# A decoder layer's kernel: the third group's sum of squares made earlier, the first two groups' norms and the third's operands in smaller steps of a held order

## The chip, the core and the metric

The kernel runs on one core of a Trainium2 chip. The metric is the time of one execution on the device in microseconds (us). The core has a matrix engine (TensorE, here PE, with PEld for the loading of its weights), a vector engine (VectorE, DVE), a scalar engine (ScalarE, ACT), a general engine (GpSimd, POOL), and a queue (SyncE, SP) that here issues nearly all transfers (DMA) between device memory and the core's memory.

## What is computed

One layer of a decoder over 2048 tokens of width 1024. A projection feeds a gated linear recurrence (HGRN2, 4 heads of 128) and a stick-breaking attention (8 heads of 64); each half's output is normalised, and both go through one output projection. A feed-forward network (FFN) and a gated embedding follow.

```python
def reference(x, p, attn_pre_norm, w_in, ...):
    h = x
    ...
        u = rmsnorm(h, attn_pre_norm[i])
        proj = u @ w_in[i]
        ...
        o_hg = hgrn2_mix(hq, hf, hi, lb_all[i])
        o_hg = rmsnorm(o_hg.astype(x.dtype), hg_out_norm[i]) * jax.nn.silu(hg)
        o_sb = stick_breaking_mix(...).reshape(B, T, SB_WIDTH)
        o_sb = rmsnorm(o_sb, sb_out_norm[i])
        mix = jnp.concatenate([o_hg, o_sb], axis=-1) @ w_out[i]
        h = h + rmsnorm(mix, attn_post_norm[i])
        u = rmsnorm(h, ffn_pre_norm[i])
        gate, up = jnp.split(u @ w_gate_up[i], [D_FF], axis=-1)
        y = (jax.nn.silu(gate) * up) @ w_down[i]
        h = h + rmsnorm(y, ffn_post_norm[i])
        h = h + (p[i] @ ple_proj[i]) * jax.nn.sigmoid(h @ ple_gate[i])
    return h
```

The change touches what lies around `mix` and the two lines after it: the sum of squares of `o_sb`, the operands of the output projection, and the norm behind it.

## The kernel before

The tokens are worked in four groups of 512 (`NG`), each as four tiles of 128 (`TT`). A product in 32-bit floats is made of three passes of PE (`mm3`, L221 to L223): the high part of one operand with the high part of the other, and the two mixed ones. `split` (L207, L208) makes the two parts: a cast on ACT gives the high part (`uh`, `wh`), and a subtraction on DVE or POOL (`V`, `G`) the low one (`ul`, `wl`).

The order of PE is that of the code; the stages are generators (`Stream`) that are woven into each other, a step at a time, by `weave` and `Rate`: of `(rows, 3, 1)` three steps are taken over the slots of that call. The instructions of the other engines and of SP are ordered by a scheduler, which works from the code's order and its own estimates. A call in `pin(...)` holds its instruction behind the one that was written before it for the same engine.

The stages that matter here, in order of time, with the places of the profiled execution:

- The last recurrence projection (to 1157 us): the input projection of group 3, with attention and the recurrence of group 2 (`hgrn(2)`) woven in, and the stream `loads[0]`, which fetches group 0's output (`out_load`).
- The output projections of groups 0 (1157 to 1252) and 1 (1252 to 1344), `out_proj`. Into them are woven the last attention, the recurrence of group 3 (`hgrn(3)`), in the second one also `post_mix(0)` (norm and residual of group 0) and `first_rows(2)`, which makes the first operands for group 2.
- The pair (1344 to 1437), `out_pair(2)`: the output projections of groups 2 and 3 in one, by seven products instead of eight; the products come in the order 1, 2, 6, 3, 7, 5, 4. `post_mix(1)` is woven in, and `first_operands`, which prepares the FFN.

The recurrence works by levels: chunks of 64 rows are halved again and again, and at each level POOL (`qp`) and DVE (`ks`) update two factors (L579, L581), and PE multiplies them (L542, L553); ACT copies the results (`score`, L566, L573). L448 and L452 are steps of the attention on DVE and POOL.

`square_sums` (L763 to L769) loads a tile of the attention's output (`o_s`), squares it on ACT (L766 the first into the sum `oss`, L768 the others) and adds it on POOL (L769). `tile_sums` (L774, L776) brings the sums of 512 tokens over rows into 4 columns, and `ratio` (L782 to L786) makes of them and of the recurrence's sums (`hgss`) the scale of one half against the other, in six small operations on POOL. `over_rows` (L792, L794) spreads the ratio over the partitions, and `scaled` (L798) multiplies an operand with it. In `first_rows`, `raw` is loaded (L808 the recurrence's half) and split. In `post_mix`, each tile has a norm in DVE (L938, two halves, after POOL's L273 and L276 for the root) and an addition (L939, DVE for the first half, POOL for the second) to the residual `h`; a second norm (ACT's L943) gives the FFN's input, which PE transposes (L949), ACT evicts (L953, four pieces each) and SP stores (L955). In the pair, `w_prep` (L837 to L846) brings weights and `a_prep` the operands; their combinations are made by L1086 and L1089, loads come by L1058, and other splits are L1073 and L1074.

Two pools bound what can be under way: `xt` has 8 buffers of 128x512, `ev` 12.

Of the kernel before, what the change touches and what calls it, by code (L numbers as in the profile page):

```python
# [13 lines left out]
ALU = mybir.AluOpType  # L14
# [76 lines left out]
def hybrid_block(  # L91
# [91 lines left out]
    def ev(dt=F32, name="ev", shape=(P, GT)):  # L183
        return fb.tile(list(shape), dt, tag="ev", name=name, bufs=12)
# [576 lines left out]
    def square_sums(acc, first, g, ks, new):  # L761
        for k in ks:
            raw = new()  # L763
            nc.sync.dma_start(raw, o_s[g][HH + k])
            if k == first:
                nc.scalar.activation(acc, raw, AF.Square)  # L766
            else:
                nc.scalar.activation(raw, raw, AF.Square)  # L768
                nc.gpsimd.tensor_tensor(acc, acc, raw, op=ALU.add)  # L769
# [27 lines left out]
    def scaled(k, raw, r):  # L797
        nc.vector.scalar_tensor_tensor(raw, raw, g_sb[:, k:k + 1], r, op0=ALU.mult, op1=ALU.mult)  # L798

    def first_rows(g, tt):  # L800
        acc = ev(name="oss")
        square_sums(acc, 0, g, range(HH), xt)
        yield
        r = ratio(g, tile_sums(acc))
        yield
        for k in range(HH):
            raw = xt("raw")
            nc.sync.dma_start(raw, o_s[g][k])  # L808
            tt[1, k] = split(wpool, "u", UB, raw, V if k % 2 else G)
            if k % 2:  # L810
                yield
        r = over_rows(r, "tr", xt)
        yield
        for k in range(HH):
            raw = xt("raw")
            nc.sync.dma_start(raw, o_s[g][HH + k])
            scaled(k, raw, r)
            nc.sync.dma_start(on_s[k], raw)
            tt[2, k] = split(wpool, "u", UB, raw, V if k % 2 else G)
            if k % 2:  # L820
                yield
# [105 lines left out]
    def post_mix(g, mix, tags, new):  # L927
# [3 lines left out]
        for t in range(TT):  # L931
            hs = [xt("h"), xt("h")]
            for j in range(2):
                nc.sync.dma_start(hs[j], x[g * GT + t * P:g * GT + (t + 1) * P, j * GT:(j + 1) * GT])
            r = row_rstd(mix[t])
            for j in range(2):
                d = mix[t][j]
                nc.vector.scalar_tensor_tensor(d, d, r, gb[j], op0=ALU.mult, op1=ALU.mult)  # L938
                (nc.gpsimd if j else nc.vector).tensor_tensor(hs[j], hs[j], d, op=ALU.add)  # L939
                nc.sync.dma_start(h_s[g][t * P:(t + 1) * P, j * GT:(j + 1) * GT], hs[j])  # L940
            r = row_rstd(hs)
            for j in range(2):
                nc.scalar.activation(mix[t][j], hs[j], AF.Copy, scale=r)  # L943
            yield
# [552 lines left out]
    loads = [Stream(out_load(g, res[g])) for g in range(2)]  # L1497
    spent = 11
    for n, (kind, g, att_n, hg_n) in enumerate(plan):
# [12 lines left out]
            0: (kept_out, 14), 2: (kept_out, 14), 4: (kept_ffn, 16), 5: (kept_ffn, 16), 6: (loads[0], ND)}.get(n, (idle, 0))  # L1512
# [28 lines left out]
    for g in range(2):  # L1541
# [6 lines left out]
        else:  # L1548
            rows = Stream(first_rows(2, tto))
            weave(op, 4, rates.part(4), r3.part(4), (pm, TT, 0), (rows, 3, 1))  # L1550
            weave(op, 2, rates.part(2), r3.part(2))
            acc3 = ev(name="oss")
            square_sums(acc3, 0, 3, range(HH - 1), xt)
            weave(op, 2, rates.part(2), r3.part(2), (pm, TT // 2, 0))
            att_stream.drain()
            square_sums(acc3, 0, 3, (HH - 1,), xt)
            weave(op, 3, r3.part(3), (pm, TT, 0), (rows, 1, 1))
            ss3 = tile_sums(acc3)
            weave(op, 2, r3.part(2), (pm, TT // 2, 0), (rows, 1, 1))
            hgs[3].drain()  # L1560
            rr3 = ratio(3, ss3)
            weave(op, 3, (rows, 2, 1))
# [19 lines left out]
    weave(op, 4, (pm, TT, 0))  # L1582
# [76 lines left out]
```

## Time and profile before

| what | value |
| --- | --- |
| median of 3 runs | 2965.28 us (2963.56 to 2966.44) |
| the profiled execution | 2966.78 us |
| its span, from first to last instruction | 2965.0 us |
| mean granted clock of PE | 0.992 |
| PE busy | 2862.4 us, 97% |
| DVE, ACT, POOL busy | 71%, 53%, 47% |
| output projection of group 1 (1252 to 1344): PE busy | 75.40 of 92 us |

A group's line in the profile has the line of the kernel, the engine, the operation, its output and inputs, the shapes and the count; behind the bar stand the busy time, the mean of one in ns, and the idle time before it with what ended it. A row in order of time begins with its start and its duration in us; in brackets stands how long the engine was idle before it and which engine, name and line ended that. "Waits" list how long an engine waited for what: in total, how often, and the longest.

### The profile page before, as it was taken

What the parts mean: (1) busy time and instruction counts of PE and PEld (TensorE: products, weight loads), DVE (VectorE), ACT (ScalarE), POOL (GpSimd) and SP (SyncE); (2) the same over time, 40 slices, a digit from 0 to 9 for tenths busy, and PEclk for the clock granted to TensorE, in tenths of its full rate; (3) what the DMA queues carried; (4) which work ended last, traced back from release to release, by engine and by line L of the source; (5) the groups of instructions that cost most, each with busy time, mean ns of one, the idle gap of its engine ahead of it and who ended that gap; (6) DMA issues with size and microseconds to landing.
All of it is one profiled execution on the core that took longest, in us unless ns stands there. A gap on an engine that the chain in (4) does not pass through costs nothing. (4 is left out here: it accounts for less than half of the span.)

```text
span 2965.0 us, 51986 instructions
## 1 busy us (share of the span) xinstructions
PE 2862.4 (97%) x17796; PEld 2397.8 (81%) x17796; DVE 2114.2 (71%) x3051; ACT 1581.2 (53%) x3220; POOL 1387.7 (47%) x1384
## 2 busy tenths in 40 slices
PE   9999999999999999988999999999999999999999
PEld 7878888877888788877788778788888888888777
DVE  4776777777788777756977777756877765666685
ACT  5667657666667666765623333455433233545542
POOL 3345456545665666764433211355722121456653
PEclk9999999999999999999999999999999999999999
DMA  7785576456556454448986787867965555677975
GB/s 230 234 257 169 173 222 207 143 168 211 182 184 183 147 155 131 142 146 310 331 283 211 253 275 265 269 204 226 325 217 174 177 172 174 214 221 236 329 253 168
DMA packets 487561, 635.27 MB, mean 214 GB/s; under 512 B 45184, under 2 KB 275584, under 8 KB 487296
## 3 DMA queue, kind: packets, MB, share of 16 engines
q1 hardware_dynamic: 487296, 631.95, 67.5%
q8 instruction: 141, 2.31, 0.3%
q14 instruction: 124, 1.02, 0.1%
HBM read 459.29 MB, written 172.49 MB: 213 GB/s over the span
## 5 line engine op out<-in xcount | busy, mean ns | idle before, releaser
L1073 ACT CAST wh<-wr 128x512 fp32r<-128x512 f32 x592 | 347.1, 618 | 501.0 <-PE mm L222 110.5
L1074 POOL TENSOR_TENSOR wl<-wr,wh 128x512 fp32r<-128x512 f32 x256 | 370.2, 1454 | 439.8 <-ACT wh L1073 390.6
L452 POOL TENSOR_TENSOR a<-be,ring 128x512 f32<-128x512 f32 (+2 forms) x320 | 325.5, 1018 | 410.0 <-DVE ring L448 382.9
L1074 DVE TENSOR_TENSOR wl<-wr,wh 128x512 fp32r<-128x512 f32 x336 | 303.4, 911 | 159.4 <-ACT wh L1073 136.4
L221 PE MATMUL mm<-uh,wh 128*128 128x512 f32 x968 | 401.4, 415 | 7.9 <-DVE vv L365 4.4
L223 PE MATMUL mm<-uh,wl 128*128 128x512 f32 x968 | 380.5, 393 | 0.0
L222 PE MATMUL mm<-ul,wh 128*128 128x512 f32 x968 | 380.2, 393 | 0.0
L448 DVE TENSOR_TENSOR_SCAN ring<-z,ring,be 128x512 f32<-128x512 f32 x192 | 245.6, 1279 | 88.2 <-ACT z L434 83.5
L221 PE MATMUL mm<-wh,uh 128*128 128x256 f32 (+1 forms) x840 | 262.4, 312 | 2.9 <-DVE eb L351 2.2
L222 PE MATMUL mm<-wl,uh 128*128 128x256 f32 (+1 forms) x840 | 249.4, 297 | 4.1 <-POOL wl L208 2.6
L223 PE MATMUL mm<-wh,ul 128*128 128x256 f32 (+1 forms) x840 | 248.7, 296 | 0.0
L433 ACT ACTIVATE be<-z 128x512 f32<-128x512 f32 (+2 forms) x320 | 171.1, 535 | 100.6 <-DVE z L431 60.9
L465 DVE TENSOR_TENSOR al<-tr,ah 128x512 fp32r<-128x512 f32 (+1 forms) x320 | 191.6, 599 | 43.7 <-ACT ah L463 42.1
L221 PEld LDWEIGHTS mm<-uh,wh 128*128 128x128 f32 x968 | 183.5, 190 | 43.4 <-issue 3.8
L223 PEld LDWEIGHTS mm<-uh,wl 128*128 128x128 f32 x968 | 182.5, 189 | 41.2
L207 ACT CAST wh<-wr 128x512 fp32r<-128x512 f32 x256 | 158.6, 619 | 102.4 <-PE mm L222 51.1
L463 ACT CAST ah<-tr 128x512 fp32r<-128x512 f32 (+1 forms) x320 | 167.8, 524 | 84.6 <-PE tr L460 83.0
L208 POOL TENSOR_TENSOR wl<-wr,wh 128x512 fp32r<-128x512 f32 x128 | 171.5, 1340 | 78.8 <-ACT wh L207 58.7
L222 PEld LDWEIGHTS mm<-ul,wh 128*128 128x128 f32 x968 | 183.4, 190 | 30.4
L460 PE MATMUL tr<-ident,a 128*128 128x128 f32 x1088 | 178.4, 276 | 19.5 <-POOL a L452 19.5
L427 PE MATMUL z<-kt,q 128*128 128x512 f32 (+3 forms) x640 | 189.4, 377 | 0.0
L1074 POOL TENSOR_TENSOR wl<-s,wh 128x512 fp32r<-128x512 f32 x40 | 62.2, 1557 | 269.8 <-ACT wh L1073 224.9
(387 smaller groups left out, 7598.3 us busy)
## 6 DMA issues: line engine op xcount, KB each, us to landing
wr<-in_w_gate_up_dram SPq DMA_DIRECT2D x292, 256.0 KB, 4.3
wr<-in_w_in_dram SPq DMA_DIRECT2D x224, 256.0 KB, 3.3
wr<-hid_s SPq DMA_DIRECT2D x154, 256.0 KB, 3.1
wr<-in_w_down_dram SPq DMA_DIRECT2D x110, 256.0 KB, 3.6
wr<-h_s SPq DMA_DIRECT2D x96, 256.0 KB, 4.5
wr<-wd_s SPq DMA_DIRECT2D x88, 256.0 KB, 3.1
kt<-k_s SPq DMA_DIRECT2D x80, 256.0 KB, 3.2
vt<-v_s SPq DMA_DIRECT2D x80, 256.0 KB, 3.3
```

The lines of the kernel that those rows point to most:

```text
L208: (lo_engine or nc.gpsimd).tensor_tensor(lo, src, hi.bitcast(F32), op=ALU.subtract)
L221: nc.tensor.matmul(o, l[0], r[0], start=start, stop=False)
L222: nc.tensor.matmul(o, l[0], r[1], start=False, stop=False)
L223: nc.tensor.matmul(o, l[1], r[0], start=False, stop=stop)
L427: nc.tensor.matmul(z[:, :n], st["q"][i][:, tb * P:(tb + 1) * P], ch["k"][:, :n], start=i == 0, stop=i == 1)
L433: nc.scalar.activation(be[:, :n], z[:, :n], AF.Sigmoid, scale=0.125)
L448: nc.vector.tensor_tensor_scan(r[:, o:o + n][:, ::-1], z[:, :n][:, ::-1], be[:, :n][:, ::-1], init, op0=ALU.mult, op1=ALU.bypass)
L452: nc.gpsimd.tensor_tensor(a[:, :n], be[:, :n], r[:, o + 1:o + n + 1], op=ALU.mult)
L460: nc.tensor.transpose(tr[:, tb * P:(tb + 1) * P], ch["a"][tb][:, sb * P:(sb + 1) * P], ident)
L465: nc.vector.tensor_tensor(lo[:, lo_c:], tr[:, lo_c:], hi[:, lo_c:].bitcast(F32), op=ALU.subtract)
L1073: nc.scalar.copy(hi, src)
L1074: lo_engine.tensor_tensor(lo, src, hi.bitcast(F32), op=ALU.subtract)
```

## The change

- A new generator `row_sums` makes the sum of squares of a group's attention output in four steps of one tile each and a fifth for the sums over rows. That of group 2 runs in the stream of the last recurrence projection, behind `out_load(0)`; the stream there takes 13 steps instead of 8. That of group 3 stays in the output projection of group 1, and its sum lies in a buffer of `xt` instead of `ev`.
- `first_rows` begins with the ratio, and makes its four operands and its four scaled operands in single steps, not in pairs.
- The squares (L766, L768), the high part of the recurrence's operands, the scalings (L798) and the norm (L938) are pinned.
- `post_mix` has three steps for each tile's norm instead of one, within the same slots; its transposes begin two slots earlier.

No instruction is added or removed on any engine.

```diff
@@ square_sums
-                nc.scalar.activation(acc, raw, AF.Square)
+                pin(nc.scalar.activation(acc, raw, AF.Square))
             else:
-                nc.scalar.activation(raw, raw, AF.Square)
+                pin(nc.scalar.activation(raw, raw, AF.Square))
                 nc.gpsimd.tensor_tensor(acc, acc, raw, op=ALU.add)
...
     def scaled(k, raw, r):
-        nc.vector.scalar_tensor_tensor(raw, raw, g_sb[:, k:k + 1], r, op0=ALU.mult, op1=ALU.mult)
+        return nc.vector.scalar_tensor_tensor(raw, raw, g_sb[:, k:k + 1], r, op0=ALU.mult, op1=ALU.mult)
+
+    sums = {}
+
+    def row_sums(g, new):
+        acc = new("oss")
+        for k in range(HH):
+            square_sums(acc, 0, g, (k,), xt)
+            if k < HH - 1:
+                yield
+        yield
+        sums[g] = tile_sums(acc)
 
     def first_rows(g, tt):
-        acc = ev(name="oss")
-        square_sums(acc, 0, g, range(HH), xt)
-        yield
-        r = ratio(g, tile_sums(acc))
+        r = ratio(g, sums[g])
         yield
         for k in range(HH):
             raw = xt("raw")
             nc.sync.dma_start(raw, o_s[g][k])
-            tt[1, k] = split(wpool, "u", UB, raw, V if k % 2 else G)
-            if k % 2:
-                yield
+            tt[1, k] = split(wpool, "u", UB, raw, V if k % 2 else G, placed=pin)
+            yield
         r = over_rows(r, "tr", xt)
         yield
         for k in range(HH):
             raw = xt("raw")
             nc.sync.dma_start(raw, o_s[g][HH + k])
-            scaled(k, raw, r)
+            pin(scaled(k, raw, r))
             nc.sync.dma_start(on_s[k], raw)
             tt[2, k] = split(wpool, "u", UB, raw, V if k % 2 else G)
-            if k % 2:
-                yield
+            yield
...
@@ post_mix, first loop over the tiles
             r = row_rstd(mix[t])
+            yield
             for j in range(2):
                 d = mix[t][j]
-                nc.vector.scalar_tensor_tensor(d, d, r, gb[j], op0=ALU.mult, op1=ALU.mult)
+                pin(nc.vector.scalar_tensor_tensor(d, d, r, gb[j], op0=ALU.mult, op1=ALU.mult))
                 (nc.gpsimd if j else nc.vector).tensor_tensor(hs[j], hs[j], d, op=ALU.add)
                 nc.sync.dma_start(h_s[g][t * P:(t + 1) * P, j * GT:(j + 1) * GT], hs[j])
+                if j == 0:
+                    yield
...
-    loads = [Stream(out_load(g, res[g])) for g in range(2)]
+    def last_loads():
+        yield from out_load(0, res[0])
+        yield from row_sums(2, lambda name: ev(name=name))
+
+    loads = [Stream(last_loads()), Stream(out_load(1, res[1]))]
...
-            0: (kept_out, 14), 2: (kept_out, 14), 4: (kept_ffn, 16), 5: (kept_ffn, 16), 6: (loads[0], ND)}.get(n, (idle, 0))
+            0: (kept_out, 14), 2: (kept_out, 14), 4: (kept_ffn, 16), 5: (kept_ffn, 16), 6: (loads[0], ND + HH + 1)}.get(n, (idle, 0))
...
             rows = Stream(first_rows(2, tto))
-            weave(op, 4, rates.part(4), r3.part(4), (pm, TT, 0), (rows, 3, 1))
-            weave(op, 2, rates.part(2), r3.part(2))
-            acc3 = ev(name="oss")
-            square_sums(acc3, 0, 3, range(HH - 1), xt)
-            weave(op, 2, rates.part(2), r3.part(2), (pm, TT // 2, 0))
+            weave(op, 4, rates.part(4), r3.part(4), (pm, 3 * TT, 0), (rows, 2, 1))
+            squares = Stream(row_sums(3, xt))
+            weave(op, 2, rates.part(2), r3.part(2), (pm, TT // 2, 0), (rows, 2, 1))
+            weave(op, 2, rates.part(2), r3.part(2), (pm, TT // 2, 0), (squares, HH - 1, 1))
             att_stream.drain()
-            square_sums(acc3, 0, 3, (HH - 1,), xt)
-            weave(op, 3, r3.part(3), (pm, TT, 0), (rows, 1, 1))
-            ss3 = tile_sums(acc3)
+            weave(op, 3, r3.part(3), (pm, TT // 2, 0), (squares, 1, 1), (rows, 2, 1))
+            squares.drain()
             weave(op, 2, r3.part(2), (pm, TT // 2, 0), (rows, 1, 1))
             hgs[3].drain()
-            rr3 = ratio(3, ss3)
-            weave(op, 3, (rows, 2, 1))
+            rr3 = ratio(3, sums[3])
+            weave(op, 3, (rows, 4, 1))
             rows.drain()
...
     weave(op, 1)
-    weave(op, 4, (pm, TT, 0))
+    weave(op, 4, (pm, 3 * TT, 0))
```

What the scheduler makes of this is read from the order of each engine's instructions. The lines of the changed kernel are shifted: `post_mix`'s L938 and L939 are L945 and L946 in it, its L953 and L955 are L962 and L964, L846 is L852, and L1058, L1074, L1086 and L1089 are L1067, L1083, L1095 and L1098. Numbers behind a name tell buffers apart.

The first place is POOL in the output projection of group 1, at the recurrence's levels (the third to the fifth L579 of a run); before:

```order
L579 TENSOR_TENSOR qp<-qp,tree 128x32x8
L782 TENSOR_SCALAR rq<-rq 128x4
L783 TENSOR_TENSOR rq<-rq,neghalf 128x4
L208 TENSOR_TENSOR ul<-raw,uh 128x512
L579 TENSOR_TENSOR qp<-qp,tree 128x16x16
L939 TENSOR_TENSOR h<-h,mix 128x512
L784 TENSOR_TENSOR rq<-rq,hgss 128x4
L452 TENSOR_TENSOR a<-be,ring_212 128x512
L579 TENSOR_TENSOR qp<-qp,tree 128x8x32
```

And after:

```order
L579 TENSOR_TENSOR qp<-qp,tree 128x32x8
L273 TENSOR_SCALAR ssum<-ss 128x1
L276 TENSOR_TENSOR rstd_17362<-ssum,neghalf 128x1
L579 TENSOR_TENSOR qp<-qp,tree 128x16x16
L452 TENSOR_TENSOR a<-be,ring_212 128x512
L579 TENSOR_TENSOR qp<-qp,tree 128x8x32
L946 TENSOR_TENSOR h<-h,mix 128x512
L208 TENSOR_TENSOR ul<-raw,uh 128x512
L579 TENSOR_TENSOR qp<-qp,tree 128x4x64
```

The ratio's steps L782, L783 and L784 have gone from between the levels, the low part (L208) and the residual's addition stand a level or two later, and a root (L273, L276) has come in.

The second place is ACT in the same stage, where it copies the scores of a set of levels (L566, L573); before:

```order
L566 COPY score_224<-small_228 32x4x32 x4
L690 ACTIVATE mix<-mm,rg 128x256 x2
L768 ACTIVATE xt<-xt 128x512
L953 ACTIVATE xt<-tr,g_ffn 128x128 x4
L207 CAST uh<-raw 128x512 x2
L207 CAST wh<-wr 128x512
L573 COPY score_224<-hg 32x4x32 x2
```

And after:

```order
L566 COPY score_224<-small_228 32x4x32 x4
L690 ACTIVATE mix<-mm,rg 128x256 x2
L962 ACTIVATE xt<-tr,g_ffn 128x128 x4
L768 ACTIVATE xt<-xt 128x512
L207 CAST wh<-wr 128x512
L207 CAST uh<-raw 128x512
L573 COPY score_224<-hg 32x4x32 x2
```

One cast of an operand (`uh`) instead of two stands between the two copies, and the square comes behind the eviction.

The third place is SP in the pair, at the loads of `o_s` for product 7; before:

```order
L940 DMA h_s_88<-h 128x512
L1058 DMA wr<-o_s_0_142 128x512
L940 DMA h_s_88<-h 128x512
L955 DMA u_s_100<-wr 128x4x128
L1058 DMA wr<-o_s_1_143 128x512
L1058 DMA wr<-u_s_99 128x512
L955 DMA u_s_100<-wr 128x4x128
L1058 DMA wr<-u_s_99 128x512
L837 DMA uh<-wo_p_123 128x512
L837 DMA ul<-wo_p_123 128x512
L1058 DMA wr<-o_s_2_144 128x512
```

And after, where the stores of `h` shown are those of the tile before the last:

```order
L947 DMA h_s_88<-h 128x512
L1067 DMA wr<-o_s_0_142 128x512
L1067 DMA wr<-o_s_1_143 128x512
L947 DMA h_s_88<-h 128x512
L964 DMA u_s_100<-wr 128x4x128 x2
L1067 DMA wr<-u_s_99 128x512 x2
L1067 DMA wr<-o_s_2_144 128x512
L1067 DMA wr<-o_s_3_145 128x512
L843 DMA uh<-wo_p_123 128x512
```

All four loads of `o_s` stand ahead of the product's weights (`wo_p`), two of them stood behind some before.

## The prediction

> **What bounds the kernel now.** I read the totals first, then the busy time of every engine stage by stage (a row gives the stretch and its length, then for each engine the busy time and its instructions, and behind them the granted clock of PE, the share of the DMA engines and GB/s), then what the matrix engine (PE) waited for in the stages that the change touches, and last the rows around each wait.
>
> ```profile
> span 2965.0 us, 51986 instructions
> PE 2862.4 (97%) x17796; PEld 2397.8 (81%) x17796; DVE 2114.2 (71%) x3051; ACT 1581.2 (53%) x3220; POOL 1387.7 (47%) x1384
> 1040.00:1157.00 117.00, 113.30 (x1079) 96.44 (x1078) 90.05 (x133) 82.30 (x173) 75.75 (x91) 0.99 0.50 148
> 1205.00:1252.00 47.00, 42.60 (x562) 37.87 (x562) 35.26 (x54) 32.74 (x69) 37.30 (x43) 1.00 0.48 149
> 1252.00:1344.00 92.00, 75.40 (x897) 69.76 (x897) 53.51 (x87) 60.27 (x149) 62.54 (x76) 0.98 0.53 168
> 1344.00:1426.00 82.00, 69.99 (x307) 55.75 (x306) 59.38 (x88) 51.44 (x124) 30.34 (x29) 0.92 0.84 291
> ```
>
> PE is busy for 97% of the span, and the change keeps every instruction, so only time in which PE stands still or runs slowly can be won. It is short in the last recurrence projection (117 less 113.3 is 3.7 us) and long behind it: 4.4 us in the second half of the output projection of group 0, 16.6 in that of group 1 and 12.0 in the first half of the pair's, 33.0 us in all. The granted clock of 0.98 and 0.92 costs 2% of 75.4 and 8% of 70.0 on top, some 7 us. So 40 us is the ceiling. PE's waits (total, times, longest), first in the stage of group 0:
>
> ```profile
> PE hg L553 <- POOL qp L579: 2.3, 1, 2.3
> ```
>
> Then the stage of group 1, where L579 is POOL's work on a level of the recurrence and L573 ACT's copy of its scores:
>
> ```profile
> PE hg L542 <- DVE ks L581: 3.9, 2, 2.2
> PE hg L553 <- POOL qp L579: 3.1, 2, 1.6
> PE hg L586 <- ACT score L573: 3.0, 1, 3.0
> PE hg L542 <- POOL qp L579: 2.2, 2, 1.5
> PE mm L222 <- POOL wl L208: 2.1, 1, 2.1
> ```
>
> And the pair:
>
> ```profile
> PE av L222 <- DVE wl L846: 5.8, 1, 5.8
> PE z L223 <- DVE ul L208: 3.2, 2, 2.7
> PE mm L222 <- DVE ul L846: 1.5, 1, 1.5
> ```
>
> No wait is long; in nearly each PE stands for a small operation of another engine that had something not urgent ahead of it. What stands ahead is what the change reorders.
>
> **The change, part by part.** *Group 2's squares leave the projection of group 0.* Four squares, three POOL adds (L769), four sums and a copy go into the last recurrence projection, and the ratio (L782 to L786) to the start of group 1's.
>
> ```profile
> 1222.04 1.29 POOL L769 TENSOR_TENSOR oss<-oss,xt 128x512 f32<-128x512 f32 x1
> 1251.02 0.98 DVE L938 SCALAR_TENSOR_TENSOR mix<-mix,rstd,gb 128x512 f32<-128x512 f32 x1
> 1253.99 1.44 DVE L581 TENSOR_TENSOR ks<-ks,pd 128x256 f32<-128x256 f32 x1
> 1267.38 0.52 POOL L782 TENSOR_SCALAR rq<-rq 128x4 f32<-128x4 f32 x1
> 1267.98 1.40 POOL L783 TENSOR_TENSOR rq<-rq,neghalf 128x4 f32<-128x4 f32 x1
> ...
> 1271.77 1.28 POOL L939 TENSOR_TENSOR h<-h,mix 128x512 f32<-128x512 f32 x1
> 1273.01 0.65 POOL L784 TENSOR_TENSOR rq<-rq,hgss 128x4 f32<-128x4 f32 x1
> ```
>
> The recurrence goes through levels; POOL makes each one's `qp` (L579), and PE waits for it. Of the 2.3 us wait in the stage of group 0 the add at 1222.04 was 1.29, which goes: 1.3. In group 1's stage L782 and L783 (1.92 us) stood ahead of the level for which PE waited first, and L939 and L784 (1.93) ahead of the next; the two waits are the 3.1 of the table, 1.6 at most each. In the new order none of the ratio's steps stands there, and L939 has gone behind them, so both waits go: 3.1. Of the other two POOL waits (2.2 together) I take a third, 0.8, as POOL comes there earlier but the same operations stay.
>
> *Group 1's norm (L938) pinned and cut into steps.* The first of the two waits for `ks` (3.9 less the longest, 2.2: 1.7 us) ends with the L581 that starts at 1253.99, behind two norm steps and their addition (L938, L938, L939) in DVE's order. In the new one a tile's norm stands behind this L581, but ahead of the next level's: two steps of up to 0.98 and an addition are over 2 us, more than the 1.7 won here. The wait mostly moves on by a level: 0.4, between -0.6 and 1.7. The other one, 2.2 us at 1298, would not be won:
>
> ```profile
> 1296.95 0.84 POOL L579 TENSOR_TENSOR qp<-qp,pd 128x256 f32<-128x256 f32 x1
> 1297.06 1.01 DVE L581 TENSOR_TENSOR ks<-ks,pd 128x256 f32<-128x256 f32 x1
> ```
>
> POOL's half of the same level ends at 1297.79, DVE's at 1298.07: DVE freed, the wait passes to POOL, 0.3 us on. I take 0.
>
> *Operands and scalings in single steps, the high parts pinned.*
>
> ```profile
> 1311.80 0.63 ACT L768 ACTIVATE xt<-xt 128x512 f32<-128x512 f32 x1 [0.99 <-DMA xt<-o_s]
> 1312.33 1.13 ACT L953 ACTIVATE xt<-tr,g_ffn 128x128 f32<-128x128 f32 x4
> 1313.44 0.62 ACT L207 CAST uh<-raw 128x512 fp32r<-128x512 f32 x1
> 1315.52 0.62 ACT L207 CAST uh<-raw 128x512 fp32r<-128x512 f32 x1 [1.46 <-DMA raw<-o_s]
> 1316.57 0.90 ACT L573 COPY score<-hg 32x128 f32<-32x128 f32 x3
> ```
>
> ACT's copy of `score` at 1316.57, for which PE waits 3.0 us, stood behind two casts of operands, and the second waited 1.46 us for its load. Both operands were made in one step; in single steps one cast stands ahead of the copy. From 1313.44 to 1316.57 are 3.1 us; less one cast the copy comes 2.5 earlier: 2.5, and 0.5 of the clock lost after it. Bounds: 1.5 (the wait for the load alone) and 4.4 (the wait and all of the clock's 1.5). For the 2.1 us on POOL's `wl` the ratio's steps of group 3 stay ahead, only in a gap where POOL waits for a cast: 1.0 of 0 to 2.1.
>
> *The pair.* Here the norm of group 1 lies between operands:
>
> ```profile
> 1350.07 0.75 DVE L938 SCALAR_TENSOR_TENSOR mix<-mix,rstd,gb 128x512 f32<-128x512 f32 x1
> 1350.73 0.69 DVE L846 TENSOR_TENSOR ul<-wr,uh 128x512 fp32r<-128x512 f32 x1
> 1353.40 0.63 PE L222 MATMUL z<-ul,uh 128*128 128x512 f32 x1
> 1353.82 0.63 PE L223 MATMUL z<-uh,ul 128*128 128x512 f32 x1
> 1356.61 0.39 PE L222 MATMUL mm<-ul,uh 128*128 128x512 f32 x1
> 1366.34 1.42 DVE L938 SCALAR_TENSOR_TENSOR mix<-mix,rstd,gb 128x512 f32<-128x512 f32 x2 [0.77 <-POOL rstd L276]
> 1368.27 1.76 DVE L1074 TENSOR_TENSOR ul<-wr,uh 128x512 fp32r<-128x512 f32 x1
> 1399.22 0.69 DVE L1086 TENSOR_TENSOR wr<-wr,wl 128x512 f32<-128x512 f32 x1 [2.77 <-DMA wr<-o_s]
> ```
>
> The 1.5 us wait ends with L846 at 1350.73; without the norm step ahead of it, 0.7 is won. Behind it matmuls took 0.63 us and started 0.42 apart (1353.40, 1353.82) where one at full clock took 0.39 (1356.61). The clock's 5.6 us of this stage (8% of 70.0), shared out over its stalls (5.8, 3.2 and 1.5) by length, give 0.8 to this one; I take it as won. The 5.8 us wait stays: where the wait of 0.77, two norm steps (1.42) and L1074 (1.76) stand ahead of its `wl` now, 3.95 us, the new order has three low parts (L208, 0.7 each as L846 at 1350.73), L1074 and a subtraction (L1086): 2.1 + 1.1 (between 0.7 and 1.76) + 0.7 is 3.9. So 0, between -1.5 and +2.
>
> The stall at product 7 (3.2 us in two waits) hangs on loads of `o_s`. On SP they stood among the last tile's stores of `h`, two of them behind operands that wait for buffers; DVE waited 2.77 us for the first. In the new order all four stand ahead of those operands and of the last tile's stores, but the norm of that tile (two L938 of 0.75 and an addition) falls between the subtractions. I take 2.0 of 3.2, and 0.5 of the 1.7 that the same sharing gives for the clock; bounds -1 and 4.9.
>
> [...]
>
> *What it costs.* Three adds and the ratio come on POOL earlier, four squares on ACT:
>
> ```profile
> L769 POOL TENSOR_TENSOR oss<-oss,xt 128x512 f32<-128x512 f32 x6 | 8.5, 1417 | 0.1
> L768 ACT ACTIVATE xt<-xt 128x512 f32<-128x512 f32 x6 | 3.7, 622 | 2.6 <-DMA xt<-o_s 2.6
> ```
>
> In the projection POOL is busy 75.75 of 117 us and ACT 82.3, so 4.3 us (three adds) and 2.5 (four squares) fit; what PE lost there was 3.7 us, and I charge 1.0 (0 to 4.3, every add on the path). The four loads stand on SP among those of weights; nothing in the rows says that those were late, 0. Group 3's squares stay in group 1's stage, now pinned on ACT, where six waited 2.6 us for loads: 1.5 (0 to 2.6). Its transposes on PE start two slots earlier, beside the same work: 0.
>
> Sum: 1.3 + 3.1 + 0.8 + 0.4 + 3.0 + 1.0 + 1.5 + 2.5 = 13.6, less 2.5, is 11.1. The profiled execution took 2966.78 us (span 2965.0), 1.5 above the median of 2965.28. From 2966.8 that gives 2955.7, from the median 2954.2; I take 2955.
>
> **Rivals.** *The waits pass on.* At 1298 the next engine is 0.3 us behind the one freed; if it is so at the levels and at `score`, only the 1.3 and some 1.5 of the others stay, from the median: about 2963. For it: four engines are 60 to 80% busy in these stages. Against it: PE's 3.1 and 2.3 us at the levels are put down to POOL alone, and of POOL's work there half is what goes.
>
> *Slower.* The pinned squares become the heads of ACT's queue: eight of them, each behind a load. One such, at 1311.80, waited 0.99 us, with the copy of `score` behind it. If PE stands 3.0 us and loses 1.5 of clock for each that is late, 4.5 us, three cancel what is won, and five make 2955 + 22.5 = 2977. It decides from four on (2973). Against it: of 2.6 us that six squares waited, PE showed one stall.
>
> *More than this.* All of the waits in the three tables but the 5.8 and the one at 1298 go, 27.1 less 8.0 is 19.1, and with 5 of the 7 us of clock, less the 2.5 charged, about 21.6: 2944.
>
> *Nothing is moved.* Excluded: the rows of the new order show the squares in the projection.
>
> **How the numbers follow.** Less than 0.2% (5.9 us) can hardly be told from no change. The forecast of 2955 (2949 to 2959) has 0.50, the waits passed on 0.26, slower 0.13, more than this 0.11. Faster is 0.50 + 0.11 = 0.61, no change 0.26, slower 0.13. The range leaves out the slower case and about half of the fuller one, 0.19, and takes in the bounds of the costs: 2943 to 2968.
>
> **What would show it.** PE's waits for `qp` and `ks` between 1205 and 1280 fall from about 7 to below 2 us; that for `score` to below 1; the busy share of PE in the stage of group 1 rises from 82% to near 90%. In the pair the 5.8 us stays, the one at product 7 halves. The last projection keeps its 117 us within 1. Wrong would be: `ks` in the place of `qp` in the waits, a square with a wait for `xt` ahead of PE's longest stall, or a last projection longer by 3 us and more.

## The result and the profile after

The changed kernel takes 2953.15 us (median of 4 runs, 2949.42 to 2956.01), the kernel before in the same comparison 2965.86 (4 runs, 2963.56 to 2970.29): a ratio of 0.9947, 95% interval 0.9933 to 0.9962. Run again among the experiments, it was 2953.03 beside 2966.33, 0.9955 (0.9941 to 0.9969). Forecast were 2955 and a range of 2943 to 2968. The time is right; about half of the places from which it was to come are not.

The totals, and three of the stretches shown of before (stretch and length, then busy time and instructions of PE, PEld, DVE, ACT and POOL, PE's granted clock, the share of the DMA engines, GB/s):

```profile
span 2953.3 us, 51991 instructions
PE 2857.0 (97%) x17796; PEld 2394.2 (81%) x17796; DVE 2115.5 (72%) x3051; ACT 1579.2 (53%) x3220; POOL 1387.6 (47%) x1384
...
1205.00:1252.00 47.00, 42.48 (x534) 37.91 (x533) 38.24 (x58) 30.07 (x66) 36.43 (x40) 1.00 0.40 124
1252.00:1344.00 92.00, 80.97 (x847) 74.53 (x846) 51.47 (x84) 60.13 (x148) 57.79 (x69) 0.96 0.64 209
1344.00:1426.00 82.00, 71.34 (x303) 57.33 (x302) 68.05 (x100) 54.73 (x135) 21.00 (x23) 0.92 0.85 290
```

PE's busy share in the projection of group 1 went from 82% to 88%. Since the later stages now begin up to 13 us earlier, the same stretch holds more of the pair; the waits show more. PE's waits in the changed kernel (total, times, longest), at the end of group 0's projection (1205 to 1245):

```profile
PE hg L553 <- POOL qp L579: 1.4, 1, 1.4
```

In group 1's, first the recurrence's upper levels (1245 to 1268):

```profile
PE hg L542 <- POOL qp L579: 2.3, 2, 1.6
PE hg L542 <- DVE al L465: 1.4, 1, 1.4
PE hg L553 <- DVE ks L581: 0.9, 1, 0.9
```

then the rest of it (1268 to 1332):

```profile
PE hg L586 <- ACT score L573: 1.8, 1, 1.8
PE mm L222 <- POOL wl L208: 1.8, 1, 1.8
PE tr L958 <- DVE al L465: 1.2, 1, 1.2
PE hg L542 <- DVE ks L581: 1.1, 2, 0.9
```

and in the pair (1332 to 1425):

```profile
PE z L223 <- DVE ul L208: 6.4, 2, 5.0
PE av L222 <- DVE wl L852: 2.2, 1, 2.2
PE av L221 <- ACT wh L851: 2.0, 1, 2.0
```

Of the two waits for `qp` that held 3.1 us, one of 0.9 for `ks` is left; the wait for `al`, a step of the attention on DVE, has grown from 0.6 to 1.4, and the stall at product 7 (`z`) from 3.2 to 6.4.

**Where the time went.** PE runs the same matmuls in nearly the same order in every kernel here, so one can count: the n-th first-pass matmul (L221) is the same work; names and shapes agree for all 3656 of them. Counted from 0, number 976 opens the stretch of the last recurrence projection, and number 1160 lies in group 0's projection, just behind it. In the profiled execution of before, and in that of after:

```profile
936.25 0.40 PE L221 MATMUL mm<-uh,wh 128*128 128x512 f32 x1
...
1162.93 0.28 PE L221 MATMUL mm<-wh,uh 128*128 128x256 f32 x1
```

```profile
932.14 0.40 PE L221 MATMUL mm<-uh,wh 128*128 128x512 f32 x1
...
1155.62 0.28 PE L221 MATMUL mm<-wh,uh 128*128 128x256 f32 x1
```

From the one to the other were 226.7 us, and are 223.5: 3.2 less. In this way for each stretch, named by its times in before (us longer or shorter than there, one profiled execution each; E1 to E12 are the experiments):

| kernel | 18-936 | 936-1163 | 1219-1251 | 1251-1288 | 1288-1318 | 1318-1345 | 1345-1404 | 1404-1434 | from 1434 |
| --- | --- | --- | --- | --- | --- | --- | --- | --- | --- |
| changed | -4.2 | -3.2 | -1.4 | -3.3 | -0.8 | -0.6 | -4.9 | +3.5 | +3.1 |
| changed, again (E5) | -1.3 | -3.2 | -1.4 | -3.3 | -1.6 | -3.4 | -3.7 | +2.0 | +1.8 |
| E1 move alone | -3.6 | +0.1 | -1.4 | +0.8 | -1.7 | -0.7 | +3.0 | -0.1 | -1.5 |
| E2 norm alone | -2.4 | -1.6 | +1.3 | -1.4 | +2.2 | -0.1 | -7.1 | +12.3 | +5.2 |
| E3 operands alone | -1.3 | -1.7 | +0.5 | +1.6 | +1.0 | -1.0 | +0.3 | +0.3 | +2.0 |
| E4 no pins | -5.0 | +1.1 | -1.4 | +6.0 | -0.4 | -1.5 | -1.5 | -3.0 | +7.8 |
| E6 pair's norm old | -2.8 | -3.1 | -1.4 | -3.3 | -1.6 | -3.4 | -0.9 | -0.9 | +1.6 |
| E7 no move | -4.0 | -1.6 | -1.4 | +8.2 | -3.7 | -3.7 | -3.0 | +2.8 | +1.5 |
| E8 operands old | -0.7 | -3.2 | -1.4 | -3.0 | -1.1 | +1.4 | -7.7 | +6.4 | +4.0 |
| E9 norm not pinned | -0.4 | -3.2 | -1.4 | +1.8 | -0.8 | -3.4 | +0.1 | -1.9 | +9.4 |
| E10 squares not pinned | -3.6 | +3.9 | -1.4 | -3.3 | -1.2 | -3.6 | -3.9 | +2.1 | +1.5 |
| E11 E6 and other buffers | -1.7 | -3.2 | -1.4 | -3.3 | -2.0 | -2.9 | -10.6 | +2.5 | +7.2 |
| E12 move, pinned squares | -3.4 | -3.2 | -1.4 | +1.4 | -1.8 | -2.2 | +2.7 | -1.3 | +2.2 |

Left out is 1163 to 1219, within 0.1 in all. Up to 936 the order of PE, ACT, DVE and POOL is that of before; the differences there (-0.4 to -5.0, every kernel) are those of single executions, and before's profiled one was slow in that stretch, as it was quick behind 1434 (all but E1 are longer there). Behind 1434 the next 94.5 us are equal in all but E8 (1.2 longer), and from 1566 on the order of the four engines is again that of before, so these differences too are taken for those of single executions. What the change did lies between: -10.7 and -14.6 us in its two profiled executions, mean -12.7; 1.6 of each belongs to before's execution, as the account of the last projection below shows.

### The profile page after: what moved, and what is told of

Read it like the earlier page. It is cut to its first block, busy times and chain, and to the rows that moved or that the text cites. A ratio compares the mean times of both kernels' runs of the same rounds, so it can differ in the third digit from the quotient of the medians.

```text
span 2953.3 us, 51991 instructions
## 1 busy us (share of the span) xinstructions
PE 2857.0 (97%) x17796; PEld 2394.2 (81%) x17796; DVE 2115.5 (72%) x3051; ACT 1579.2 (53%) x3220; POOL 1387.6 (47%) x1384
## 5 line engine op out<-in xcount | busy, mean ns | idle before, releaser
L1083 POOL TENSOR_TENSOR wl<-wr,wh 128x512 fp32r<-128x512 f32 x256 | 369.0, 1449 | 452.6 <-ACT wh L1082 411.8
L1083 DVE TENSOR_TENSOR wl<-wr,wh 128x512 fp32r<-128x512 f32 x336 | 298.3, 895 | 162.9 <-ACT wh L1082 137.2
L221 PE MATMUL mm<-uh,wh 128*128 128x512 f32 x968 | 400.6, 414 | 5.1 <-DVE vv L365 2.5
L221 PE MATMUL mm<-wh,uh 128*128 128x256 f32 (+1 forms) x840 | 262.1, 312 | 2.2 <-DVE eb L351 2.2
L221 PEld LDWEIGHTS mm<-uh,wh 128*128 128x128 f32 x968 | 183.3, 189 | 40.6 <-DVE eb L351 2.2
L208 POOL TENSOR_TENSOR wl<-wr,wh 128x512 fp32r<-128x512 f32 x128 | 172.0, 1343 | 77.1 <-ACT wh L207 57.1
L1083 POOL TENSOR_TENSOR wl<-s,wh 128x512 fp32r<-128x512 f32 x40 | 66.8, 1672 | 267.1 <-ACT wh L1082 229.8
```

The source lines that it names most:

```text
L208: (lo_engine or nc.gpsimd).tensor_tensor(lo, src, hi.bitcast(F32), op=ALU.subtract)
L221: nc.tensor.matmul(o, l[0], r[0], start=start, stop=False)
L1083: lo_engine.tensor_tensor(lo, src, hi.bitcast(F32), op=ALU.subtract)
```

## The experiments

All were timed against the kernel before in five rounds. Single executions of any of the kernels scatter over 5 to 22 us, so the ratios have intervals of 0.11% to 0.18% to each side. The table by stretches shows where the time went, for one execution each.

### The parts alone (E1, E2, E3)

E1, the squares of group 2 moved, nothing pinned, no step cut:

```diff
+    def last_loads():
+        yield from out_load(0, res[0])
+        yield from row_sums(2, lambda name: ev(name=name))
...
-            0: (kept_out, 14), 2: (kept_out, 14), 4: (kept_ffn, 16), 5: (kept_ffn, 16), 6: (loads[0], ND)}.get(n, (idle, 0))
+            0: (kept_out, 14), 2: (kept_out, 14), 4: (kept_ffn, 16), 5: (kept_ffn, 16), 6: (loads[0], ND + HH + 1)}.get(n, (idle, 0))
...
```

> Only the first part: group 2's squares and sums run in the last recurrence projection, the first operands begin with the ratio; no step is cut, nothing newly pinned, group 3 as before. If the time was won because the adds and the ratio no longer stand between the recurrence's levels on POOL (the prediction's terms of 1.3 and 3.1, and 3.2 us that the changed kernel won in the last projection itself), this gives 5 to 8 us of the 12.7: 2958 to 2961 beside a kernel before of 2966, with the last projection shorter by about 3 us. If the gain is the held order's, it is within 2 us of before.

Measured: 2963.9 us, 0.9993 (0.9977 to 1.0010). The last projection did not get shorter (+0.1), the levels (1251 to 1288) neither (+0.8): there PE waits 2.7 us for `ks` where it waited for `qp`. The add that stood ahead of a level in group 0's projection is gone, -1.4. The first theory fails for the move by itself.

E2, the norms of groups 0 and 1 in three steps, L938 pinned:

```diff
             r = row_rstd(mix[t])
+            yield
...
-                nc.vector.scalar_tensor_tensor(d, d, r, gb[j], op0=ALU.mult, op1=ALU.mult)
+                pin(nc.vector.scalar_tensor_tensor(d, d, r, gb[j], op0=ALU.mult, op1=ALU.mult))
...
```

> Only the norms of groups 0 and 1: three steps for each tile, L938 pinned, in the same slots as before. By the prediction's sum this part is worth 0.4 (the wait for ks) and in the pair 1.5 plus 2.5 at product 7, so about 4 us: 2962. By the changed kernel's trace the pair wins 4 us up to product 7 and gives them back there: then 0, 2966.

Measured: 2971.38 us, 1.0018 (1.0002 to 1.0035), the one kernel slower than before. It wins 7.1 us in the pair and gives back 12.3, where PE's transposes (L952 in this kernel) wait for the last tile's second norm (L946 in it; 1340 to 1440):

```profile
PE tr L952 <- ACT mix L946: 12.1, 1, 12.1
PE hg L952 <- ACT mix L946: 3.1, 1, 3.1
```

E3, the operands of group 2 in single steps, casts and scalings pinned:

```diff
-            tt[1, k] = split(wpool, "u", UB, raw, V if k % 2 else G)
-            if k % 2:
-                yield
+            tt[1, k] = split(wpool, "u", UB, raw, V if k % 2 else G, placed=pin)
+            yield
...
-            scaled(k, raw, r)
+            pin(scaled(k, raw, r))
...
```

> Only the operands of group 2 in single steps, with the casts and the scalings pinned; its squares stay where they were. The prediction's term for the copy of score was 3.0 and for the last low part of the weights 1.0: about 4 us, 2962, and PE's 3.0 us wait for score falls to 1 or less. If the wait only passes on, 1 us or less: 2965.

Measured: 2967.45 us, 0.9998 (0.9983 to 1.0013): no change. PE's wait for `score` fell to 2.3 us. The three parts, alone, come to -0.07, +0.18 and -0.02%; the whole change gives -0.5%. None of the three has the pins on the squares; those are tried by E10 and E12.

### The whole again, and with parts undone (E5, E7, E8)

E5 is the changed kernel unaltered.

> The changed kernel once more, with the kernel before in the same rounds, since single executions of either scatter by 10 us and the first comparison had four of each. If its gain is real, the ratio lies between 0.993 and 0.997; if the four were lucky, it is above 0.998. The sum of the three parts tried alone was within 0.1% of no change, so a gain here is one that only the parts together give.

Measured: 2953.03 us, 0.9955 (0.9941 to 0.9969). The gain is real, and none of E1, E2 and E3 gives it alone. Later runs hold more of it: E12, the move with pinned squares and nothing else, gives 0.30%, and E6, without the pair's part of the norm, all of it.

E7 leaves group 2's squares, sums and ratio where they were:

```diff
-        r = ratio(g, sums[g])
+        acc = ev(name="oss")
+        square_sums(acc, 0, g, range(HH), xt)
+        yield
+        r = ratio(g, tile_sums(acc))
...
```

> The changed kernel with group 2's squares, sums and ratio where they were. By the prediction's terms the waits at the levels return, 1.3 and 3.1 us, and the 3 us that the changed kernel won in the last projection go as well: 5 to 8 us slower than the changed one, 2958 to 2961. If the move is worth what it was alone (0.07%), 2 us: 2955.

Measured: 2962.23 us, 0.9989 (0.9977 to 1.0000), 9 us slower than the changed kernel, more than either theory had. The levels take 8.2 us more than before, since PE now waits for the sum itself (1250 to 1285):

```profile
PE tr L774 <- POOL oss L769: 6.6, 1, 6.6
```

PE's order is that of the code, and pinned squares come later than free ones: ACT begins them between 1249.5 and 1251.0 here, and between 1216.2 and 1227.4 in before. With the pins in place the move is needed, as the move (E1) needs pins.

E8 has group 2's operands in pairs again, without pins on casts and scalings:

```diff
-            tt[1, k] = split(wpool, "u", UB, raw, V if k % 2 else G, placed=pin)
-            yield
+            tt[1, k] = split(wpool, "u", UB, raw, V if k % 2 else G)
+            if k % 2:
+                yield
...
-            pin(scaled(k, raw, r))
+            scaled(k, raw, r)
...
```

> The changed kernel with the operands of group 2 in pairs, their casts and scalings not pinned. By the prediction's terms PE's wait for the copy of score grows from 1.8 to 3 us and that for the weights' last low part stays: 2 to 4 us slower than the changed one. By the part alone (no change, and the wait for score fell by 0.7): within 1 us of the changed one.

Measured: 2956.88 us, 0.9967 (0.9956 to 0.9979). Beside E5, 1318 to 1345 is 4.8 us longer. PE's waits there (1300 to 1340), then E5's (1300 to 1332):

```profile
PE mm L222 <- POOL wl L208: 2.1, 1, 2.1
...
PE mm L221 <- ACT mix L690: 0.7, 1, 0.7
```

```profile
PE mm L222 <- POOL wl L208: 1.1, 1, 1.1
...
PE mm L221 <- ACT mix L690: 0.3, 1, 0.3
```

The waits make only 1.4 of the 4.8 us. In the rest PE ran slower, as the same stretch in E8 and then in E5 shows (PE's busy time stands behind the length of the stretch, its granted clock ahead of the last two figures):

```profile
1309.10:1337.50 28.40, 25.61 (x192) 25.20 (x191) 13.80 (x23) 12.91 (x32) 13.45 (x15) 0.88 0.67 218
```

```profile
1307.50:1331.10 23.60, 22.28 (x188) 21.87 (x187) 12.51 (x22) 12.25 (x30) 13.43 (x15) 1.00 0.71 235
```

The changed kernel's first execution, the same kernel as E5, had 24.59 us busy here at a clock of 0.89, and its stretch is 2.8 us longer than E5's. So one execution does not tell how much of the 4.8 the operands gave; the ratios of E8 and E5 are 0.12% (3.6 us) apart, and their intervals overlap.

### The pins (E4, E9, E10, E12)

E4 is the changed kernel without any of its new pins.

```diff
-                pin(nc.scalar.activation(acc, raw, AF.Square))
+                nc.scalar.activation(acc, raw, AF.Square)
...
-                pin(nc.vector.scalar_tensor_tensor(d, d, r, gb[j], op0=ALU.mult, op1=ALU.mult))
+                nc.vector.scalar_tensor_tensor(d, d, r, gb[j], op0=ALU.mult, op1=ALU.mult)
...
```

> The changed kernel with none of its new pins: squares, casts, scalings and norms are placed freely, all steps as in the change. If the steps do the work, it is as fast as the changed kernel, 2953 within 2 us. If holding the order does, most of the gain goes: 2960 or more.

Measured: 2961.63 us, 0.9987 (0.9972 to 1.0003). Without the pins the levels take 6.0 us more than before and the last projection 1.1 more. The steps without the pins do not do it.

E10 takes off only the squares' pins, the first line of the diff above and its like.

> The changed kernel with the squares' pins alone taken off. The last projection was 3.2 us shorter than before wherever squares moved into it were pinned, and 1 longer where they were not. If the pins of the squares give that, this kernel loses 3 to 4 us there: 2957; the levels from 1251 to 1288 keep their 3.3. If it loses nothing there, the 3.2 come from something else.

Measured: 2957.44 us, 0.9963 (0.9949 to 0.9977). The last projection takes 3.9 us more than before where the changed kernel takes 3.2 less; the levels keep their -3.3. ACT's rows there, and POOL's, in order of time, with PE's waits (940 to 1163) behind them:

```profile
1011.79 0.63 ACT L768 ACTIVATE xt<-xt 128x512 f32<-128x512 f32 x1 [2.71 <-DMA xt<-o_s]
1012.33 0.60 ACT L207 CAST wh<-wr 128x512 fp32r<-128x512 f32 x1
```

```profile
1013.01 1.26 POOL L208 TENSOR_TENSOR wl<-wr,wh 128x512 fp32r<-128x512 f32 x1 [1.44 <-ACT wh L207]
1014.23 1.02 POOL L579 TENSOR_TENSOR qp<-qp,pd 128x256 f32<-128x256 f32 x1
```

```profile
PE hg L542 <- POOL qp L579: 5.5, 3, 3.5
```

A square stands at the head of ACT's queue 2.71 us ahead of its data; behind it waits a cast of weights, behind that POOL's low part, behind that the level's `qp`, and PE stands 3.5 us for it. With the pins the same wait is 0.5 (1010 to 1022 in the changed kernel):

```profile
PE hg L542 <- POOL qp L579: 0.5, 1, 0.5
```

ACT begins the four free squares between 976.4 and 1055.7, the pinned ones between 1071.6 and 1123.1, and none of the pinned ones waits for its load. Of the 7.1 us between the two kernels 4.0 are waits of PE (10.2 us in the stretch beside 6.2), and the rest is matmuls that ran slower (220.4 us busy beside 217.3). Free squares do not cost as much in every kernel: +0.1 in E1 and +1.1 in E4. By the ratios E10 lies 0.08% (2 us) behind E5, with intervals that overlap.

E9 takes off only the norm's pin (L938, the last line of E4's diff).

> The changed kernel with L938's pin alone taken off; steps, squares and operands as in the change. Without any pins the stretch from 1251 to 1288 us (the recurrence's levels in the projection of group 1) was 6.0 us longer than before, in the changed kernel 3.3 shorter. If the norm's place sets this, the stretch is longer again by 6 to 9 us and the last projection keeps its 3.2: about 2959. If the squares' pins set it, this is 2953.

Measured: 2958.41 us, 0.9973 (0.9957 to 0.9989). The last projection keeps its -3.2; the levels take 1.8 us more than before, 5.1 more than with the pin. PE's waits there (1248 to 1285), and DVE's rows:

```profile
PE hg L542 <- POOL qp L579: 3.1, 2, 1.6
PE hg L553 <- DVE ks L581: 2.8, 1, 2.8
```

```profile
1261.44 1.79 DVE L945 SCALAR_TENSOR_TENSOR mix<-mix,rstd,gb 128x512 f32<-128x512 f32 x2 [1.69 <-POOL rstd L276]
1263.15 1.11 DVE L208 TENSOR_TENSOR wl<-wr,wh 128x512 fp32r<-128x512 f32 x1
1264.19 1.76 DVE L946 TENSOR_TENSOR h<-h,mix 128x512 f32<-128x512 f32 x1
1265.87 1.27 DVE L448 TENSOR_TENSOR_SCAN ring<-z,ring,be 128x512 f32<-128x512 f32 x1
...
1267.24 0.41 DVE L581 TENSOR_TENSOR ks<-ks,tree 128x256 f32<-128x256 f32 x1
```

DVE stands 1.69 us for a root that POOL has not made, and then does the norm's two halves, a low part, the addition and a scan before the `ks` for which PE waits. In each kernel with the squares moved and the norm free (E1, E4, E9, E12) `ks` has the place that `qp` had; with the norm pinned and the squares moved the levels are 3.0 to 3.3 shorter in all (changed, E5, E6, E8, E10, E11).

E12 is E1 with the squares pinned.

> The kernel before with group 2's squares moved and all squares pinned; norms and operands as before. Without the pins this part won 0.07%. If the pins make the last projection shorter, 3 us more are won there: 2961. If the move needs the norm's new places too, the levels in the projection of group 1 stay as long as before or longer, and the whole stays 8 us behind the changed kernel.

Measured: 2960.28 us, 0.9970 (0.9957 to 0.9983). The last projection gets its -3.2, the levels stay 1.4 longer than before. Both outcomes hold: E1 and E12 differ in the squares' pins alone, and 3.3 us lie between them in the last projection; and 4 us to the changed kernel are still missing by the ratios, 7 by the medians.

### The pair (E6, E11)

E6 has the pair's norm as before; that of group 0 stays cut and pinned.

```diff
-    def post_mix(g, mix, tags, new):
+    def post_mix(g, mix, tags, new, fine=True):
...
-            yield
+            if fine:
+                yield
...
-    weave(op, 4, (pm, 3 * TT, 0))
+    weave(op, 4, (pm, TT, 0))
...
```

> The changed kernel, but in the pair the norm of group 1 is as before: one step for a tile, not pinned; in the projection of group 1 it stays cut. The norm alone made the pair 7 us shorter up to its third product and 12 longer at product 7 (in the profiled execution). If the pinned norm is what holds up product 7, this kernel loses PE's 5.0 and 1.4 us there and is 2 to 4 us faster than the changed one, 2950. If the norm between the operands costs more than it delays, the wait for the second product's low part returns to 5 us and it is 3 us slower, 2956.

Measured: 2951.72 us, 0.9947 (0.9930 to 0.9965). Product 7's stretch is 0.9 us shorter than before where the changed kernel's is 2.0 and 3.5 longer, and PE waits 0.6 us for `ul` there instead of 6.4; the stretch ahead of it loses 3 to 4 of its gain. In all it is as good as the changed kernel. Both theories saw half. PE's two longest waits in the pair (1330 to 1425):

```profile
PE av L221 <- ACT wh L851: 3.0, 1, 3.0
PE av L222 <- DVE wl L852: 2.3, 1, 2.3
```

Both are for the last weights of the second product. They came through four buffers, and the last load went out when one came free. E11 is E6 with two of the blocks in the wide buffers:

```diff
-            raw = wpool.tile([P, GT], F32, tag="wr", name="wr", bufs=4)
+            raw = slot("wr", 0, "wr") if prod == 2 and k > 1 else wpool.tile([P, GT], F32, tag="wr", name="wr", bufs=4)
```

> The changed kernel with the pair's norm as before (2951.7 measured), and the last two of the four weight blocks of the pair's second product loaded into the wide buffers instead of the four that were still held. In that kernel PE waited 3.0 us for the cast of the last block and 2.3 for its low part, since its load was issued only when a buffer came free. If the buffer is what bounds it, the two waits fall below 2 us together and the time to about 2948. If the transfers are the bound (380 GB/s in that stretch), the wait moves to the operands that load behind: no change, 2952.

Measured: 2949.96 us, 0.9938 (0.9920 to 0.9955), the best median of all. Both waits are gone and the pair up to product 7 is 10.6 us shorter than before; some of it comes back, now with waits for transfers (1330 to 1425; the two longest):

```profile
PE z L222 <- DMA ul<-wo_p: 3.0, 4, 2.1
PE z L223 <- DVE ul L208: 2.0, 2, 1.8
```

So the buffer bounded those waits of E6, and behind it the transfers do. Its interval overlaps that of the changed kernel; by the stretches it is 6.5 us better in the pair (-8.1 beside -1.4 and -1.7), by the ratios 5, by the medians 3.

## Why the prediction was right, and where it was not

Mean of the changed kernel's two profiled executions, beside the terms:

| stretch | forecast | measured |
| --- | --- | --- |
| last projection | +1.0 | -3.2 |
| group 0, the add (1219-1251) | -1.3 | -1.4 |
| levels (1251-1288): 3.1, 0.8, 0.4 | -4.3 | -3.3 |
| the wait at 1298 and `score` (1288-1318), `score`'s clock and `wl` (1318-1345) | -4.0 | -3.2 |
| pair to product 7 (1345-1404) | -1.5 | -4.3 |
| product 7 (1404-1434) | -2.5 | +2.7 |
| group 3's squares | +1.5 | in the others |
| sum | -11.1 | -12.7 |

That the sum came within 2 us is in part luck: the last projection is 4.2 us better than forecast and the pair up to product 7 2.8, and product 7 is 5.2 worse.

- *The cost in the last projection* had the wrong sign. It was priced by how much POOL and ACT had to do; what mattered was where a square with late data stood in ACT's order, as E10 (7.1 us) and E12 beside E1 (3.3 us) show. The gain itself is smaller than the 3.2 of the table. E2, E3 and E7, in which the order of PE, ACT, DVE and POOL up to here is that of before, are also 1.6 to 1.7 shorter, since before's profiled execution ran some of these matmuls slower (219.4 us busy, 217.8 in those three, 217.3 in the changed kernel). Beside them the pinned move is worth 1.6.
- *The add ahead of a level* is right: the wait went from 2.3 to 1.4, the stretch by 1.4.
- *The levels* are right in kind and 1.0 short. The two waits of 3.1 behind the ratio's operations went, and 0.9 came up for `ks`; the first wait for `ks` (1.6) went too, where 0.4 was forecast, and 0.8 of it came up for `al`; the third of 2.2 (0.8) was not won, the two waits are 2.3. The pin on the norm, to which the prediction gave nearly nothing, is what keeps the rest from passing on to DVE: 5.1 us between E9 and the changed kernel.
- *`score`* is right in kind and too large. The wait fell from 3.0 to 1.8 in one execution and 0.8 in the other, so 1.2 and 2.2 were won of 2.5. That two casts held the copy is not borne out. In E1 two casts of operands stand ahead of it, neither waits for its load, and PE waits 0.9; in E3 one stands there (at 1315.92) for whose load ACT waits 1.21, and PE waits 2.3. In the changed kernel the square of group 3 stands ahead of the copy. Its row and that of the next cast of an operand, then the square's in E5:

```profile
1302.35 0.63 ACT L768 ACTIVATE xt<-xt 128x512 f32<-128x512 f32 x1 [1.68 <-DMA xt<-o_s]
...
1303.83 0.62 ACT L207 CAST uh<-raw 128x512 fp32r<-128x512 f32 x1 [0.34 <-DMA raw<-o_s]
```

```profile
1304.59 0.64 ACT L768 ACTIVATE xt<-xt 128x512 f32<-128x512 f32 x1 [1.07 <-DMA xt<-o_s]
```

ACT stood 2.0 us for loads ahead of the copy in the one execution and 1.07 in the other, and PE's waits differ by the same 1.0. So by the rows it was late loads in ACT's order, not the number of casts; no run changes the loads alone.

- *The wait at 1298* was forecast to pass on. That for `ks` fell from 2.2 to 1.1, and in the same stretch 1.2 came up for `al` and 0.6 for `qp`.
- *`wl` and the clock behind `score`*: the wait for `wl` fell from 2.1 to 1.8 and 1.1. The stretch won 0.6 us in one execution and 3.4 in the other, and most of that difference is the clock (0.89 and 1.00), so the 0.5 that was forecast for it is no fixed sum.
- *The pair's second product*: forecast 0 for the 5.8 us wait, measured 4.2 in two waits, within the bounds given (up to 2). E11 shows that in E6 a buffer of the weights bounded it, which the prediction had not seen. Of the 4.3 us that the pair won up to product 7, 2.4 are matmuls that ran faster (52.2 us busy before, 49.8 after), where 0.8 was forecast.
- *Product 7* had the wrong sign. The loads were issued early, as forecast; DVE's order decided, with the norm that the prediction saw fall between the subtractions but priced too low. In E6, with that norm as before, 0.6 of the 6.4 us is left. DVE's rows in the changed kernel, between the subtraction of the third operand (1386.22) and its low part (1394.89):

```profile
1388.02 1.78 DVE L945 SCALAR_TENSOR_TENSOR mix<-mix,rstd,gb 128x512 f32<-128x512 f32 x1
...
1390.34 1.75 DVE L1098 TENSOR_TENSOR wr<-wr,wl 128x512 f32<-128x512 f32 x1
1392.01 2.36 DVE L1083 TENSOR_TENSOR ul<-wr,uh 128x512 fp32r<-128x512 f32 x2
...
1394.89 0.67 DVE L208 TENSOR_TENSOR ul<-wr,uh 128x512 fp32r<-128x512 f32 x1
```

A norm, an operand of product 5 (L1098) and two of the FFN (L1083) stand ahead, none of them due, and two of those took more than twice the 0.67 us of the row that ends the list.

Of the rivals, the waits did pass on, in the kernels with one part (E1, E2, E3) and without the pins (E4); in the whole 1.7 us of the levels did, and 1.8 came up in the stretch of 1298. The slower one, a square at the head of ACT's queue, is a true mechanism, and the unpinned squares of group 2 paid for it most (3.5 us in E10); the pinned one of group 3 paid for it ahead of `score`.

Of the signs named ahead, PE's busy share in group 1's stage came near (88%). The waits for `qp` and `ks` between 1205 and 1280 fell from 10.1 us, where the prediction had counted about 7, to 5.1 and not below 2; that for `score` came below 1 in one execution of two; the stall at product 7 doubled instead of halving; and `ks` in the place of `qp`, a sign of being wrong, is there with 0.9 us.

## What to carry to other kernels

Where each engine works down a fixed order, look at every engine that feeds a wait: at the levels the pinned move alone (E12) lost 1.4 us and the norm alone (E2) won 1.4, and both in the changed kernel won 3.3. Price a moved operation not by its duration but by when its data come and what stands behind it in the queue; holding it back was worth more than starting it early for the squares (4.0 us of waits in the last projection, E10 beside the changed kernel). Read the difference of two traces from the same instruction to the same instruction, and first over a stretch that the change doesn't touch: 4 of 12 us lay there. Nor were the matmuls that ran slow in before's last projection (219.4 us busy beside 217.8 in E2, E3 and E7) the change's doing: compare with other runs in which that stretch is unchanged.

## What the runs showed of the hardware

The clock's loss behind a short wait is not fixed by the wait. At the same place, behind the same wait for `qp`, before's execution, then E3's:

```profile
1016.78 0.46 PE L542 MATMUL hg<-qp,ks 128*32 128x32 f32 x32 [2.00 <-POOL qp L579]
...
1018.00 0.63 PE L221 MATMUL mm<-uh,wh 128*128 128x512 f32 x1
```

```profile
1015.61 0.46 PE L542 MATMUL hg<-qp,ks 128*32 128x32 f32 x32 [2.03 <-POOL qp L579]
...
1016.80 0.40 PE L221 MATMUL mm<-uh,wh 128*128 128x512 f32 x1
```

After 2.00 us the matmuls took 0.63 us, after 2.03 they took 0.40. In before the granted clock was 1.00 from 1012.67 to 1016.78 and 0.50 from 1018.00 to 1021.26; behind a wait of 1.57 us at 1078.56 it was 0.50 once more, from 1079.46 to 1082.66. Half of these 3.26 and 3.20 us is some 1.6 us lost each time. E2, E3 and E7 have the same order here and the same wait of 2.0 us at the first place, and PE is 217.8 us busy in them from 936 to 1163 where it is 219.4 in before: one such loss less.

In the changed kernel's rows at product 7, DVE's operations of 128x512 took 0.67 to 0.75 us where POOL was at none of that size (1385.56 to 1386.82 and 1394.29 to 1396.69). Those at 1388.02 and 1390.34, begun while POOL was at one (at 1387.60 for 1.66 us, at 1389.89 for 1.65), took 1.78 and 1.75. Not each one beside POOL's is slower: the one at 1389.73 took 0.68, and the two at 1358.88, begun while POOL was at its addition of 1358.44 (1.29), took 1.40 together. POOL's low part of weights at 1342.01, with DVE idle, took 1.29 us; one at product 7 took 1.71:

```profile
1391.50 1.71 POOL L852 TENSOR_TENSOR wl<-wr,wh 128x512 fp32r<-128x512 f32 x1
```

At the start of the pair (1330 to 1352 in the changed kernel) the transfers ran at 380 GB/s, and a load of 256 KB took 5.3 to 6.4 us to land (medians by kind of load), against 3.2 to 4.6 for the eight kinds with the most bytes over the whole:

```profile
DMA packets 4579, 8.35 MB, mean 380 GB/s; under 512 B 508, under 2 KB 508, under 8 KB 4578
```
